# Raw parked operands of x, split on landing, and three more eviction buffers in the last projection phases of a hybrid encoder layer

## The chip, the cores and the metric

The kernel runs on one core of one Trainium2 chip. A core has a matrix engine (PE, with PEld for its weight loads), a vector engine (DVE), a scalar engine (ACT), a general engine (POOL), and a queue processor (SP) that issues the DMA transfers. Each engine works through its own list in order and waits where an instruction's inputs or buffers are not ready. The metric is device time in microseconds, the median of several runs; less is better. Before the change it is 1917.55 us (three runs, 1917.55 to 1919.67).

## What is computed

One layer on 2048 frames of a new stream and on 64 frames that continue another one:

```python
h = rmsnorm(x, norm_g) @ w_in          # x: (T, 1024), w_in: (1024, 6144)
qa, ka, va, za, qb, kb, vb, zb, ga, gb = jnp.split(h, _split_points(), axis=-1)
oa = attention(qa, ka, va)             # two softmaxes, ALiBi, block-causal, a1 - lam * a2
ob = retention(qb, kb, vb)
oa = (rmsnorm(oa, subln_g) * 0.8) * silu(za)
ob = rmsnorm(ob) * silu(zb)
m = ga * (oa @ w_oa) + gb * (ob @ w_ob)
y = x + m @ w_out
```

All data are 32-bit floats. The projection by `w_in` is the largest matrix product. The outputs are `y`, the keys and values, and the retention states.

## The kernel before

**Precision.** PE multiplies operands that are rounded (type fp32r). To keep the precision, an operand is split into a high part (a rounding copy, on ACT) and a low part (operand minus high part, on DVE or POOL), and each product is three matmuls: high by high, high by low, low by high. `xh`, `xl` are the parts of x, `wh`, `wl` those of a weight.

**Stages.** The frames are projected in two halves. The first half runs to some 600 us. In the second half, `w_stream` goes through the weights in order (`natural` for keys, queries and values, then `transposed` for eleven pairs of column blocks), and the last five pairs go through `quad`. Meanwhile `z_stream` runs attention and retention. After quad, the output stage follows (its first matmuls are L2652). In the profile, `transposed` is the matmul of L1131 with 256, 288 or 512 columns, quad is L1547, and attention is L1862 to L1999.

**Quad** multiplies in the manner of Strassen: a 2 x 2 blocked product with seven block products in place of eight. So x's blocks A11, A12, A22 and the sums S1 to S4 of blocks are its operands. `PHASES` (L73) lists the seven in order: t2 with S2, b11 with A11, b21 with A12, t1 with S1, t3 with S3, t4 with A22, b22 with S4. A phase takes one operand of x (high and low part, 1.1 MB each) through the five pairs, for two groups of 256 and 288 columns: ten groups of 12 matmuls, 120 in a phase, 840 in all. Each group ends in one PSUM bank, which ACT (`q_copy`, L1574) or DVE (`q_scaled`, L1567) evicts, either into a sum kept in SBUF (`u`) or into an eviction buffer (`ev`, three of them) that is stored to DRAM (`gaT`, `gbT`). In phase t3 each group has two evictions on DVE.

**Parking.** The operands don't fit beside the rest of the second half. `x_again` writes them to DRAM (`xd`, one tensor of high and one of low parts): first A11, A12, A22, straight from `xh` and `xl`; then, in 20 chunks of 128 or 96 columns, S1 to S4: POOL adds high and low part (L1460) and forms the sums (L1463 to L1469), ACT casts them (L1492, into the one buffer `thi`), DVE subtracts (L1495, in one of the two buffers `tlo`), SP stores both. `x_pass` loads each phase's parts into one of two slots in the room of x's second segment, as soon as a slot is free; the loads stand on L1515, which the trace shows as L279, the helper `ld`. Stores are L284, the helper `st`.

**Weights.** `next_piece` takes a loaded piece of weights (`ws`, three buffers), casts it on ACT (L726), and starts a task `next_low` that subtracts the low part (L741) when the cast is done: on POOL, in quad on the less loaded of DVE and POOL. Then it waits until ACT's planned backlog is at most 0.7 us (`PACE`).

**What sets the order.** A planner runs all these generators as tasks with priorities. It keeps an estimated clock for each engine (`P`, `A`, `V`, `G`, and `ld`, `st` for transfers); a task yields the time at which it wants to go on, and the first ready task of the highest priority goes next. Instructions of PE, ACT and DVE stand in their lists as the tasks emit them; those of POOL and SP are ordered by the framework's scheduler. An estimate that is too short makes an engine wait at that place, with all that is behind it.

## Time and profile before

| | |
|---|---|
| median of three runs | 1917.55 us |
| the profiled execution | 1916.72 us, span 1914.9 us |
| busy: PE, DVE, ACT, POOL | 1879.6, 1327.4, 965.8, 667.3 us |
| PE idle in all | 35.3 us |
| mean granted PE clock | 0.995 |
| DMA | 353.45 MB, mean 185 GB/s |
| quad's matmuls | 1391.3 to 1560.6 us |

The profile is of one execution. A line of waits reads: who waited, for whom, total us, times, longest us. In lists of instructions the brackets at the end give the idle time before one and what ended it. A busy PE can still be slow: the granted clock falls after a pause, and the count of matmuls in a stretch shows that.

### The profile page before, as it was taken

Reading aid. Unit: us, or ns where it says so; the run is one execution under the profiler, and the core shown is the slowest. Engines: PE = TensorE matmul, PEld = TensorE weight load, DVE = VectorE, ACT = ScalarE, POOL = GpSimd, SP = SyncE. Lnnn points to the kernel's source line nnn. Section 1 sums busy time; section 2 is a strip of 40 time slices with the busy share of each in tenths; the row PEclk is TensorE's granted clock in tenths of the full one; section 3 lists DMA queues with packets and bytes.
Section 4 is the critical chain, followed back from the end, with each engine's and each line's share of the span. In section 5 each row is a group of like instructions: output and inputs, shape, how many; then the busy total and the mean of one; then the engine's idle time right before and its main releaser. Section 6 shows DMA issues by size and latency. Waiting matters only on the chain.

```text
span 1914.9 us, 32977 instructions
## 1 busy us (share of the span) xinstructions
PE 1879.6 (98%) x11090; PEld 1652.8 (86%) x11090; DVE 1327.4 (69%) x3089; ACT 965.8 (50%) x2242; POOL 667.3 (35%) x727
## 2 busy tenths in 40 slices
PE   9999999999998999999999999999999999999999
PEld 7788888888888889888888889889999889999887
DVE  6765756656574776876377686668787469987664
ACT  6434544545334666555355554546675246654221
POOL 2420365554651132121402263611022435532442
PEclk9999999999999999999999999999999999999999
DMA  7654456666858886564523764762744989886542
GB/s 252 216 171 135 156 157 192 185 188 198 253 158 245 249 279 186 154 179 124 152 66 105 188 172 130 188 175 73 229 136 123 295 252 288 265 260 199 179 153 78
DMA packets 409755, 353.45 MB, mean 185 GB/s; under 512 B 85617, under 2 KB 355057, under 8 KB 407794
## 3 DMA queue, kind: packets, MB, share of 16 engines
q1 hardware_dynamic: 409586, 351.35, 62.3%
q8 instruction: 88, 1.44, 0.3%
q14 instruction: 81, 0.66, 0.1%
HBM read 224.96 MB, written 125.44 MB: 183 GB/s over the span
## 4 chain that ended last, share of the span: by engine, by line
PE 58%; DMA 5%; DVE 4%; POOL 1%; issue 1%; SPq 1%; ACT 1%; DVEq 0%; POOLq 0%; ACTq 0%
PE mm L1131 19%; PE at L1974 3%; PE s L1863 2%; PE s L1862 2%; PE mm L1547 2%; PE pv L1954 2%; PE pv L1953 2%; PE pv L1952 2%; DMA gbT<-ev 1%; PE s L2776 1%; PE s L2778 1%; PE s L2777 1%; DMA gaT<-ev 1%; DMA xd<-xsl 1%; PE at L2653 1%
## 5 line engine op out<-in xcount | busy, mean ns | idle before, releaser
L741 POOL TENSOR_TENSOR wl<-ws,wh 128x512 fp32r<-128x512 f32 x106 | 140.9, 1340 | 291.6 <-ACT wh L726 204.8
L1131 PE MATMUL mm<-wh,xh 128*128 128x512 f32 x504 | 203.5, 404 | 0.0
L1131 PE MATMUL mm<-wl,xh 128*128 128x512 f32 x504 | 198.0, 393 | 1.1 <-POOL wl L741 1.1
L1131 PE MATMUL mm<-wh,xl 128*128 128x512 f32 x504 | 198.2, 393 | 0.0
L1131 PE MATMUL mm<-xh,wh 128*128 128x288 f32 (+2 forms) x544 | 180.3, 332 | 5.8 <-ACT ev L1574 5.8
L1131 PE MATMUL mm<-xh,wl 128*128 128x288 f32 (+2 forms) x544 | 176.4, 324 | 0.0
L1131 PE MATMUL mm<-xl,wh 128*128 128x288 f32 (+2 forms) x544 | 176.3, 324 | 0.0
L1902 ACT ACTIVATE row<-row,a_mx 128x1024 f32<-128x1024 f32 (+7 forms) x144 | 149.9, 1043 | 12.6 <-DVE a_mx L1881 12.6
L1990 DVE TENSOR_TENSOR atl<-at,ath 128x512 fp32r<-128x512 f32 (+1 forms) x144 | 92.6, 658 | 82.6 <-ACT ath L1988 82.2
L1988 ACT CAST ath<-at 128x512 fp32r<-128x512 f32 (+1 forms) x144 | 79.2, 564 | 116.0 <-PE at L1974 108.7
L850 POOL TENSOR_TENSOR wl<-ws,wh 128x256 fp32r<-128x256 f32 x64 | 54.2, 846 | 195.9 <-ACT wh L841 195.8
L1871 DVE CUSTOM_DVE_ANT_0 row<-s,dfar 128x512 f32<-128x512 f32 (+2 forms) x150 | 92.7, 632 | 42.2 <-PE s L1863 41.7
L1728 POOL TENSOR_TENSOR r_y<-r_y,r_sq 128x256 f32<-128x256 f32 x32 | 27.2, 849 | 264.6 <-DVE r_sq L1725 191.4
L1131 PEld LDWEIGHTS mm<-xh,wh 128*128 128x128 f32 x544 | 103.0, 189 | 12.8 <-ACT ev L1574 6.0
L1131 PEld LDWEIGHTS mm<-wh,xl 128*128 128x128 f32 x504 | 94.6, 188 | 21.6
L1131 PEld LDWEIGHTS mm<-wl,xh 128*128 128x128 f32 x504 | 95.0, 189 | 19.2 <-POOL wl L741 1.9
L1131 PEld LDWEIGHTS mm<-wh,xh 128*128 128x128 f32 x504 | 94.8, 188 | 17.6 <-DVE raw L1302 0.2
L1131 PEld LDWEIGHTS mm<-xh,wl 128*128 128x128 f32 x544 | 103.0, 189 | 7.0 <-POOL wl L741 0.3
L1131 PEld LDWEIGHTS mm<-xl,wh 128*128 128x128 f32 x544 | 103.2, 190 | 6.5
L1924 DVE SCALAR_TENSOR_TENSOR row<-row,a_w 128x1024 f32<-128x1024 f32 (+5 forms) x88 | 99.5, 1137 | 0.0
L1862 PE MATMUL s<-K,q 128*128 128x512 f32 (+3 forms) x246 | 93.1, 380 | 0.3 <-DVE a_acc L1871 0.2
L1863 PE MATMUL s<-K,q 128*128 128x512 f32 (+3 forms) x246 | 89.7, 365 | 0.0
(541 smaller groups left out, 6044.4 us busy)
## 6 DMA issues: line engine op xcount, KB each, us to landing
ws<-in_w_in_dram SPq DMA_DIRECT2D x155, 256.0 KB, 3.6
q<-qT SPq DMA_DIRECT2D x128, 128.0 KB, 3.1
K<-kT SPq DMA_DIRECT2D x48, 256.0 KB, 4.7
V<-vN SPq DMA_DIRECT2D x24, 512.0 KB, 5.2
row<-in_x_prompt_dram SPq DMA_DIRECT2D x16, 512.0 KB, 4.7
wz<-in_w_in_dram SPq DMA_DIRECT2D x32, 256.0 KB, 4.3
row<-in_cache_k_T_dram SPq DMA_DIRECT2D x32, 256.0 KB, 3.0
row<-in_cache_v_diff_dram SPq DMA_DIRECT2D x32, 256.0 KB, 3.6
```

What stands on the lines that cost most here:

```text
L741: eng.tensor_sub(l, st, h.bitcast(F32))
L850: nc.gpsimd.tensor_sub(l[:, cs], src, h[:, cs].bitcast(F32))
L1131: nc.tensor.matmul(ps, p, q, start=c == 0 and i == 0, stop=c == KC - 1 and i == 2)
L1547: nc.tensor.matmul(ps, w[:, c], x, start=c == 0 and k == 0, stop=c == 3 and k == 2)
L1862: nc.tensor.matmul(ps, q1s, kk, start=True, stop=False)
L1863: nc.tensor.matmul(ps, q2s, kk, start=False, stop=True)
L1871: nc.vector.tensor_tensor_reduce(out=row[:, k0:k0 + n], in0=ps, in1=tab, scale=-SLOPES[h], scalar=3.0e38, op0=ALU.add, op1=ALU.min, accum_ ...
L1902: nc.scalar.activation(u, u, AF.Exp, bias=mx, scale=-1.0, accum_out=lp[:, k:k + 1])
L1924: nc.vector.scalar_tensor_tensor(out=u0, in0=u1, scalar=w[:, 0:1], in1=u0, op0=ALU.mult, op1=ALU.add)
L1974: nc.tensor.transpose(at[:, w:w + 128], src, self.ident)
L1988: nc.scalar.copy(ah[:, :w], at[:, :w])
L1990: nc.vector.tensor_sub(al[:, :w], at[:, :w], ah[:, :w].bitcast(F32))
```

## The change

It edits four things.

- **Parking.** Only S2 is still split before it is stored (`xd2`). S1, S3, S4, A22, A11 and A12 are stored unsplit (`xd`, six parcels in place of twice seven). A chunk now takes one `tlo` buffer for the blocks and the `thi` buffer for the sums, both filled by POOL; ACT and DVE split S2 alone, a quarter of the elements, into an eviction buffer. A chunk's task rests 4000 ns of the planner's time (`SPREAD`) before the next.
- **Landing.** S2 is loaded in two parts into slot 0 before quad. Every other operand is loaded unsplit into `xraw`, a new buffer in the room where the sums `u` are (11 blocks of each width remain in place of 13 and 12), and then split into a slot: four casts on ACT and four subtractions on DVE, 544 columns each. The next raw load waits until this is done.
- **Eviction buffers.** Once parking is over, `q_ev` takes from `ev`, `thi` or `tlo`, whichever is free first: six buffers.
- **Weights.** Outside quad the low part is emitted on POOL right behind the cast, and the next piece is not paced.

```diff
 
 PLAIN = 11
+SPREAD = 4000.0
...
-NAMES = ("S1", "S3", "S2", "S4", "A11", "A12", "A22")
+NAMES = ("S1", "S3", "S4", "A22", "A11", "A12")
...
-        self.xd = [tc.dram_tile([128, 7, 4, 544], F32, name=f"xd{j}") for j in range(2)]
+        self.xd = tc.dram_tile([128, 6, 4, 544], F32, name="xd")
+        self.xd2 = tc.dram_tile([128, 2, 4, 544], F32, name="xd2")
...
         self.wq += new
-        self.spawn(self.next_low(st, h, l, t, new, kind), 0, "w")
-        yield self.act - PACE
-
-    def next_low(self, st, h, l, t, new, kind):
+        if kind == "quad":
+            self.spawn(self.next_low(st, h, l, t, new), 0, "w")
+            yield self.act - PACE
+        else:
+            self.next_sub(self.nc.gpsimd, self.G, st, h, l, t, new)
+            yield self.pe
+
+    def next_low(self, st, h, l, t, new):
         yield t - LAT
-        eng, cost = self.lighter() if kind == "quad" else (self.nc.gpsimd, self.G)
+        self.next_sub(*self.lighter(), st, h, l, t, new)
+
+    def next_sub(self, eng, cost, st, h, l, t, new):
         eng.tensor_sub(l, st, h.bitcast(F32))
         t = cost(512, t)
         self.give("ws", t)
         for u in new:
             u[2] = t
-        yield self.pe
...
+    def x_chunk(self, g, c, raw, sums, a, n):
         xh, xl = self.xnext[g]
-        for k, (b, j) in enumerate(((1, 1), (1, 0), (0, 0), (0, 1))):
+        for k, (b, j) in enumerate(((1, 0), (1, 1), (0, 0), (0, 1))):
             h, l = (x[:, b, 4 * j + c, a:a + n].bitcast(F32) for x in (xh, xl))
             nc.gpsimd.tensor_add(raw[:, k], h, l)
             t = self.G(n, self.pe)
-        s1, s3, s2, s4 = (raw[:, k] for k in range(4))
-        nc.gpsimd.tensor_add(s1, s1, s3)
+        a21, a22, a11, a12 = (raw[:, k] for k in range(4))
+        s1, s3, s4, s2 = (sums[:, k] for k in range(4))
+        nc.gpsimd.tensor_add(s1, a22, a21)
         self.G(n)
-        nc.gpsimd.tensor_sub(s3, s2, s3)
+        nc.gpsimd.tensor_sub(s3, a11, a21)
         self.G(n)
-        nc.gpsimd.tensor_sub(s2, s1, s2)
+        nc.gpsimd.tensor_sub(s2, s1, a11)
         self.G(n)
-        nc.gpsimd.tensor_sub(s4, s4, s2)
-        return self.G(n)
+        nc.gpsimd.tensor_sub(s4, a12, s2)
+        return t, self.G(n)
 
     def x_again(self):
...
         yield lambda: "nat1" in self.done
-        self.kept = 0
         for g, w in enumerate(WIDTH):
-            gsl = slice(256 * g, 256 * g + w)
-            for k, (b, j) in (("A11", (0, 0)), ("A12", (0, 1)), ("A22", (1, 1))):
-                for x, d in zip(self.xnext[g], self.xd):
-                    self.kept = self.st(d[:, NAMES.index(k), :, gsl], x[:, b, 4 * j:4 * j + 4, :].bitcast(F32), 600000)
-                    yield self.pe + 4000
             n = (128, 96)[g]
             for c, a in [(c, a) for c in range(4) for a in range(0, w, n)]:
                 yield from self.take("tlo")
-                l = self.sb(self.ep, [128, 512], "tlo", "xsl", F32R)[:, 0:4 * n]
-                raw = l.bitcast(F32)
-                t = self.x_chunk(g, c, raw.rearrange("p (k t) -> p k t", k=4), a, n)
+                yield from self.take("thi")
+                raw, sums = (self.sb(self.ep, [128, 512], tag, name)[:, 0:4 * n].rearrange("p (k t) -> p k t", k=4)
+                             for tag, name in (("tlo", "xa"), ("thi", "xs")))
+                t, t2 = self.x_chunk(g, c, raw, sums, a, n)
+                usl = slice(256 * g + a, 256 * g + a + n)
                 yield t
-                yield from self.take("thi")
-                h = self.sb(self.ep, [128, 512], "thi", "xsh", F32R)[:, 0:4 * n]
-                nc.scalar.copy(h, raw)
-                t = self.A(4 * n, self.pe)
+                t = self.st(self.xd[:, 3:6, c, usl], raw[:, 1:4], n << 11)
+                yield t2
+                ev, tag = yield from self.q_ev(2 * n)
+                e = ev.bitcast(F32R).rearrange("p (k t) -> p k t", k=2)
+                nc.scalar.copy(e[:, 0], sums[:, 3])
+                t3 = self.A(n, self.pe)
+                self.give("tlo", max(t, t2))
+                t4 = self.st(self.xd[:, 0:3, c, usl], sums[:, 0:3], n << 11)
+                yield t3
+                nc.vector.tensor_sub(e[:, 1], sums[:, 3], e[:, 0].bitcast(F32))
+                t = self.V(n + 100, t3)
+                self.give("thi", max(t, t4))
                 yield t
-                nc.vector.tensor_sub(l, raw, h.bitcast(F32))
-                t2 = self.V(4 * n + 100, t)
-                for d, x, tag, t in zip(self.xd, (h, l), ("thi", "tlo"), (t, t2)):
-                    if t > self.pe:
-                        yield t
-                    self.kept = self.st(d[:, 0:4, c, 256 * g + a:256 * g + a + n],
-                                        x.bitcast(F32).rearrange("p (k t) -> p k t", k=4), n << 11)
-                    self.give(tag, self.kept)
+                self.kept = self.st(self.xd2[:, :, c, usl], e.bitcast(F32), n << 10)
+                self.give(tag, self.kept)
+                yield self.pe + SPREAD
         self.parked = 1
 
     def x_pass(self):
-        self.xslots, self.xfree, self.parked = [], [(0, 0.0), (1, 0.0)], -1
+        self.xslots, self.xfree, self.parked, self.xraw = [], [(1, 0.0)], -1, None
         yield lambda: self.parked == 1 and self.seg1_done is not None
         yield max(self.seg1_done, self.kept)
-        for _, name, _ in PHASES:
+        for k, (_, name, _) in enumerate(PHASES):
+            if k == 0:
+                for j, x in enumerate(self.x_slot(0)):
+                    t = self.ld(x.bitcast(F32), self.xd2[:, j].rearrange("p c t -> p (c t)"), 1114112)
+                self.xslots.append((0, t))
+                yield lambda: self.xraw is not None
+                continue
+            t = self.ld(self.xraw, self.xd[:, NAMES.index(name)].rearrange("p c t -> p (c t)"), 1114112)
             s = yield from self.ring(self.xfree)
-            for x, d in zip(self.x_slot(s), self.xd):
-                t = self.ld(x.bitcast(F32), d[:, NAMES.index(name)].rearrange("p c t -> p (c t)"), 1114112)
-                yield self.pe
+            yield t
+            h, l = self.x_slot(s)
+            for c in range(0, 2176, 544):
+                self.nc.scalar.copy(h[:, c:c + 544], self.xraw[:, c:c + 544])
+                t = self.A(544, self.pe)
+                yield t
+                self.nc.vector.tensor_sub(l[:, c:c + 544], self.xraw[:, c:c + 544], h[:, c:c + 544].bitcast(F32))
+                t = self.V(644, t)
             self.xslots.append((s, t))
+            yield t
 
     def u_room(self):
...
         pool = self.z2.enter_context(self.tc.tile_pool(name="sums", bufs=1))
-        room = [pool.tile([128, 2304], F32, tag=f"u{k}", name=f"u{k}") for k in range(3)]
-        self.ufree = [[(x[:, n * k:n * k + n], 0.0) for x in rooms for k in range(x.shape[1] // n)]
-                      for n, rooms in ((256, (room[0], room[2][:, 0:1152])), (288, (room[1], room[2][:, 1152:2304])))]
+        self.xraw = pool.tile([128, 2176], F32, tag="xraw", name="xraw")
+        self.ufree = []
+        for n in WIDTH:
+            u = pool.tile([128, 11 * n], F32, tag=f"u{n}", name=f"u{n}")
+            self.ufree.append([(u[:, n * k:n * k + n], 0.0) for k in range(11)])
...
     def q_ev(self, n):
-        yield from self.take("ev")
-        return self.sb(self.ep, [128, 512], "ev")[:, :n]
+        tag = yield from self.either(1, "ev", *(("thi", "tlo") if self.parked == 1 else ()))
+        return self.sb(self.ep, [128, 512], tag, "ev")[:, :n], tag
...
     def q_end(self, q, ps, bank, k, t, dst, b, scale, grouped):
-        ev = yield from self.q_ev(q["n"])
+        ev, tag = yield from self.q_ev(q["n"])
...
-        self.q_put(q, dst, ev, b, grouped)
+        self.q_put(q, dst, ev, tag, b, grouped)
...
-        self.give("ev", self.st(out, ev[:, 0:256], 1 << 17))
+        self.give(tag, self.st(out, ev[:, 0:256], 1 << 17))
```

The lists are the same up to about 600 us, and hold the same matmuls behind. Three places show what moves.

*DVE, the end of attention in quad.* `atl` is the low part of attention's weights, `u` and `ev` are quad's evictions (into a sum, into a buffer). Before:

```order
L1990 TENSOR_TENSOR atl_17201<-at_17195,ath_17200 128x512
L1731 SCALAR_TENSOR_TENSOR r_o_17001<-r_o_17001,gsub_754,r_y_17003 128x256
L1990 TENSOR_TENSOR atl_17227<-at_17221,ath_17226 128x512
L1567 TENSOR_TENSOR ev_17238<-tp_17205,u2_16006 128x256
L1990 TENSOR_TENSOR atl_17253<-at_17247,ath_17252 128x512
L1990 TENSOR_TENSOR atl_17275<-at_17270,ath_17274 128x384
L1567 TENSOR_TENSOR ev_17284<-mm_17256,u2_16006 128x288
L1567 TENSOR_TENSOR u2_16006<-mm_17297,u0_16004 128x256
L1692 TENSOR_TENSOR r_sq_17316<-r_sq_17316,pv_17087 1x256
```

After:

```order
L1534 TENSOR_TENSOR xl1_124<-xraw_16428,xh1_123 128x544
L2012 TENSOR_TENSOR atl_16936<-at_16930,ath_16935 128x512
L1534 TENSOR_TENSOR xl1_124<-xraw_16428,xh1_123 128x544
L1589 TENSOR_TENSOR u256_16429<-tp_16916,u256_16429 128x256
L2012 TENSOR_TENSOR atl_16970<-at_16964,ath_16969 128x512
L2012 TENSOR_TENSOR atl_16986<-at_16980,ath_16985 128x512
L1589 TENSOR_TENSOR u288_16430<-mm_16949,u288_16430 128x288
L2012 TENSOR_TENSOR atl_17020<-at_17014,ath_17019 128x512
L2012 TENSOR_TENSOR atl_17034<-at_17029,ath_17033 128x384
L1589 TENSOR_TENSOR u256_16429<-mm_16995,u256_16429 128x256
```

The last `atl` (128x384) stood among the evictions into `ev` of phase b21; it stands now among those into `u` of phase b11, beside the split of an operand (L1534). In PE's list the last transposition of attention (L1974, now L1996) stands after 174 of quad's 840 matmuls, before after 354; 486 of its 544 stand ahead of quad, before 444.

*ACT, the last chunks of parking* (`ath` is attention's high part). Before:

```order
L1574 COPY ev_14208<-mm_14169 128x288
L1492 CAST xsh_14217<-xsl_14174 128x384
L1574 COPY ev_14251<-mm_14213 128x288
L1988 CAST ath_14292<-at_14287 128x512
L1492 CAST xsh_14296<-xsl_14264 128x384
L1988 CAST ath_14303<-at_14298 128x512
L1988 CAST ath_14339<-at_14334 128x512
L1988 CAST ath_14354<-at_14349 128x512
```

After:

```order
L1596 COPY ev_14776<-mm_14664 128x288
L1924 ACTIVATE row_6182,a_lp_14795<-row_6182,a_mx_14712 128x1024
L1924 ACTIVATE row_6182,a_lp_14795<-row_6182,a_mx_14712 128x640
L1498 CAST ev_14808<-xs_14763 128x96
L1706 COPY r_o_14813<-pv_14605 128x256
L1708 ACTIVATE r_sq_14814<-r_o_14813 128x256
L1710 ACTIVATE r_hi_14816<-r_o_14813 128x256
L1924 ACTIVATE row_6182,a_lp_14822<-row_6182,a_mx_14792 128x1024
```

The casts of four sums at once (`xsh`), which need the one buffer `thi`, are gone from between attention's casts; one cast of 96 columns into an eviction buffer is left of a chunk.

*DVE and SP in phase t3 of quad.* Before, DVE, then SP:

```order
L1567 TENSOR_TENSOR u0_16004<-s_17616,u0_16004 128x256
L1567 TENSOR_TENSOR ev_17669<-s_17616,u2_16006 128x256
L1567 TENSOR_TENSOR u1_16005<-s_17637,u1_16005 128x288
L2598 TENSOR_TENSOR on_17478<-on_17478,z_17479 128x528
L1567 TENSOR_TENSOR ev_17689<-s_17637,u1_16005 128x288
L1567 TENSOR_TENSOR u0_16004<-at_17660,u0_16004 128x256
L1567 TENSOR_TENSOR ev_17708<-at_17660,u0_16004 128x256
L1567 TENSOR_TENSOR u1_16005<-at_17682,u1_16005 128x288
L2609 TENSOR_TENSOR ogl_17681<-on_17478,ogh_17680 128x528
L1567 TENSOR_TENSOR ev_17733<-at_17682,u1_16005 128x288
```

```order
L279 DMA z_17569<-zaT_67 128x2x264
L279 DMA xh1_123<-xd0_76 128x2176
L279 DMA xl1_124<-xd1_77 128x2176
L279 DMA ws_17565<-wsum_75 128x4x128
L279 DMA on_17568<-oaT_71 128x2x264
L284 DMA gaT_69<-ev_17557 128x256
L279 DMA z_17592<-zbT_68 128x2x264
L279 DMA on_17591<-obT_72 128x2x264
L284 DMA gaT_69<-ev_17583 128x4x8
L284 DMA gaT_69<-ev_17583 128x256
```

After, DVE, then SP:

```order
L1589 TENSOR_TENSOR u256_16429<-mm_17623,u256_16429 128x256
L1534 TENSOR_TENSOR xl1_124<-xraw_16428,xh1_123 128x544
L1589 TENSOR_TENSOR ev_17655<-mm_17623,u256_16429 128x256
L1589 TENSOR_TENSOR u288_16430<-s_17646,u288_16430 128x288
L2620 TENSOR_TENSOR on_17507<-on_17507,z_17508 128x528
L1534 TENSOR_TENSOR xl1_124<-xraw_16428,xh1_123 128x544
L1589 TENSOR_TENSOR ev_17680<-s_17646,u288_16430 128x288
L1589 TENSOR_TENSOR u256_16429<-s_17669,u256_16429 128x256
L2482 TENSOR_TENSOR w_o_diffl0_17240<-wst_17580,w_o_diffh0_17239 128x2x256
L1534 TENSOR_TENSOR xl1_124<-xraw_16428,xh1_123 128x544
L1589 TENSOR_TENSOR u288_16430<-at_17697,u288_16430 128x288
L2631 TENSOR_TENSOR ogl_17685<-on_17507,ogh_17684 128x528
```

```order
L280 DMA ws_17630<-wsum_75 128x4x128
L280 DMA wst_17643<-in_w_o_ret_dram 128x2x256
L280 DMA wst_17656<-in_w_o_ret_dram 128x2x256
L280 DMA wst_17681<-in_w_o_diff_dram 128x2x256
L285 DMA gaT_69<-ev_17655 128x256
L280 DMA ws_17704<-wsum_75 128x4x128
L280 DMA ws_17725<-wsum_75 128x4x128
L285 DMA gaT_69<-ev_17680 128x4x8
L285 DMA gaT_69<-ev_17680 128x256
```

Between t3's evictions there are now the splits of the operand for t4 (L1534), and more low parts of the output weights (L2482, before L2460, behind t3): to its last eviction the list of t3 holds 20 evictions, four splits, six low parts of the output weights and two operations of the gates. On SP the pair of loads `xh`, `xl` between the stores of evictions is gone. The store of `ev_17655` stands behind the load of `wst_17681`, whose buffer is freed by the low part of `wst_17580`, six operations behind that eviction on DVE.

9 lines of the change are left out of this document (4 added, 5 removed).

## The prediction

> **What bounds the kernel now.** The page's first part comes first.
>
> ```profile
> PE 1879.6 (98%) x11090; PEld 1652.8 (86%) x11090; DVE 1327.4 (69%) x3089; ACT 965.8 (50%) x2242; POOL 667.3 (35%) x727
> ```
>
> The matrix engine (PE) is busy for 1879.6 of 1914.9 us and the change takes no product away. So only PE's 35.3 us of idle time can be won, and the slow clock that follows a long pause. I therefore asked for busy time by stage. The columns are length, then busy time of PE, PEld, DVE, ACT and POOL (instructions in brackets), PE's granted clock, DMA share and GB/s.
>
> ```profile
> 1100.00:1265.00 165.00, 158.00 (x1078) 146.00 (x1077) 109.52 (x270) 83.40 (x194) 86.69 (x154) 0.99 0.64 167
> 1265.00:1391.00 126.00, 125.94 (x842) 116.42 (x842) 100.81 (x290) 77.23 (x159) 17.76 (x15) 0.99 0.56 156
> 1391.00:1495.00 104.00, 102.45 (x786) 99.30 (x785) 82.21 (x207) 64.44 (x137) 29.01 (x24) 1.00 0.45 141
> 1495.00:1515.00 20.00, 20.00 (x162) 20.00 (x161) 9.97 (x19) 6.96 (x11) 10.14 (x7) 1.00 1.00 328
> 1515.00:1562.00 47.00, 37.75 (x258) 36.17 (x258) 27.70 (x49) 14.95 (x26) 13.05 (x11) 0.89 0.88 248
> 1562.00:1915.00 353.00, 349.10 (x2231) 316.63 (x2230) 259.28 (x408) 152.40 (x353) 144.52 (x108) 1.00 0.67 206
> ```
>
> Operands are parked in the first row, quad runs from 1391 to 1561. Its tail, after attention, loses most: 258 matmuls in 47 us, where the row above does 162 in 20 us (8.1 per us). At that rate 258 take 31.9 us, so the tail loses **15.1 us**: 9.25 us idle (47 - 37.75), 5.9 us slow clock. The parking stage is idle for 7.0 us. The chain of waits names the cause in the tail (start, length, what; the second row is SP's own, from the timeline):
>
> ```profile
> by line: DMA gbT<-ev 70.8%; PE s L1547 12.5%; SPq L279 7.1%; DVE ev L1567 7.0%; DVE u L1567 4.3%; DVE ogl L2609 3.8%; issue 3.1%; SPq L284 2.8%; DVEq L1567 0.6%
> ...
> 1521.49 1.85 SPq L279 DMA_DIRECT2D xl<-xd  x1
> ...
> 1523.43 8.51 DMA gbT<-ev
> 1532.07 0.47 DVE ev L1567
> ```
>
> From 1514 to 1540, 71% of the chain is a store of an eviction. The worst took 8.51 us from its issue, straight behind a load that SP issued at 1521.49, the second half of an operand of x. The next rows are DMA issues of 1490 to 1562 (count, KB, median us to landing), then waits of 1520 to 1562 (total, times, longest):
>
> ```profile
> gbT<-ev SPq DMA_DIRECT2D x23, 128.0 KB, 3.3
> xh<-xd SPq DMA_DIRECT2D x2, 1088.0 KB, 7.8
> xl<-xd SPq DMA_DIRECT2D x2, 1088.0 KB, 9.4
> ...
> DVE ev L1567 <- DMA gbT<-ev: 15.9, 9, 5.7
> ...
> PE s L1547 <- DVE ev L1567: 4.9, 2, 3.2
> ...
> PE s L1547 <- DVE wl L741: 2.5, 1, 2.5
> ```
>
> DVE waits nine times for one of three buffers to be stored, PE for DVE. The weight's low part on DVE is late for the same reason: it stands in DVE's list behind those evictions.
>
> **Parking.** PE's waits from 1100 to 1265, and the ACT instructions at the longest of them:
>
> ```profile
> PE pv L1952 <- ACT ath L1988: 3.4, 1, 3.4
> PE pv L1954 <- DVE atl L1990: 2.0, 2, 1.7
> PE s L2319 <- DMA row<-kbT: 1.0, 1, 1.0
> ...
> 1260.44 0.51 ACT L1492 CAST xsh<-xsl 128x384 fp32r<-128x384 f32 x1 [5.20 <-DMA xd<-xsh]
> 1260.86 1.06 ACT L1988 CAST ath<-at 128x512 fp32r<-128x512 f32 x2
> ...
> 1134.95 1.70 DVE L1495 TENSOR_TENSOR xsl<-xsl,xsh 128x512 fp32r<-128x512 f32 x1
> ...
> 1260.00:1270.00 10.00, 8.29 (x48) 7.60 (x49) 6.54 (x18) 4.07 (x9) 0.00 (x0) 0.83 0.23 61
> ```
>
> ACT stood 5.20 us before a parking cast whose one buffer was still being stored, with attention's cast behind it: 3.4 us of PE. The 1.7 us wait is the 1.70 us subtraction of a parked sum on DVE. After the pause the clock is 0.83 for 10 us, about 1.7 us more. I put parking at 3.4 + 1.7 + 1.7 = 6.8 us, and the stage with its small waits at 8.7.
>
> **The change, part by part.** *Stores of A11, A12, A22 leave* and come back as raw sums with the chunks. The traffic halves: 14 parcels of 1.1 MB were stored and loaded, now 8. The removed early stores surround this stall, which I leave in place:
>
> ```profile
> 606.56 0.61 PE L1131 MATMUL mm<-xh,wh 128*128 128x288 f32 x1 [5.78 <-ACT ev L1574]
> ...
> 598.82 3.12 SPq L279 DMA_DIRECT2D q<-qT  x4
> 602.04 0.54 SPq L284 DMA_DIRECT2D qbT<-ev  x1
> ```
>
> Its eviction's store is issued only at 602.04, behind loads of q that still stand in front of it. I take 0; the bounds are 0 and -5.8.
>
> *Splits while parking.* These are 20 casts on ACT and 20 subtractions on DVE, on a quarter of the elements now:
>
> ```profile
> L1492 ACT CAST xsh<-xsl x20: 495/516/635, 1073.6 to 1260.4; 128x384 fp32r<-128x384 f32 x12, 128x512 fp32r<-128x512 f32 x8
> L1495 DVE TENSOR_TENSOR xsl<-xsl,xsh x20: 546/622/1700, 1074.6 to 1263.5; 128x384 fp32r<-128x384 f32 x12, 128x512 fp32r<-128x512 f32 x8
> ```
>
> That is 10.3 us of ACT and 12.4 us of DVE by medians. With a quarter of the elements and some fixed part I estimate half, so 5 and 6 us go. ACT no longer waits there for a 4-operand store: the wait for the buffer moves to POOL's sums, behind which weights' low parts are queued. And each chunk holds one of the three eviction buffers for its split sum. Each chunk also rests 4 us of the planner's time. I take half of the 8.7 us as saved: **-4.3** (bounds 0 and -8.7).
>
> *Splits on landing.* Six operands, each four ACT casts and four DVE subtractions of 544 columns, 24 each. By the rows above (512 columns: ACT 0.62, DVE 0.62 to 1.70) that is 24 x 0.65 = 15.6 us of ACT and 16 to 41 us of DVE. DVE is 79% busy from 1391 to 1495 (82.21 of 104); four operands there would add at least 10 us. But attention's last transposition now stands after 174 of quad's 840 matmuls in PE's list, where it stood after 354, so less of it overlaps. In the tail, the crowded phase is t3. Its list on DVE has 20 evictions, four splits, six low parts of the output weights and two gate operations:
>
> ```profile
> L2460 DVE TENSOR_TENSOR w_o_diffl<-wst,w_o_diffh 128x512 fp32r<-128x512 f32 x5 | 6.5, 1295 | 0.0
> ...
> L2460 DVE TENSOR_TENSOR w_o_retl<-wst,w_o_reth 128x512 fp32r<-128x512 f32 x5 | 4.8, 982 | 0.0
> ...
> L1567 DVE TENSOR_TENSOR ev<-at,u 128x256 f32<-128x256 f32 (+1 forms) x10 | 4.3, 434 | 2.8 <-DMA gbT<-ev 2.8
> ...
> L2598 DVE TENSOR_TENSOR on<-on,z 128x528 f32<-128x528 f32 x4 | 2.8, 698 | 0.0
> ```
>
> The last numbers before the second bar are the mean ns of one. Evictions 20 x 0.434 = 8.7, splits 2.6 to 6.8, low parts 6 x 1.14 (mean of the two rows) = 6.8, gates 1.4: 19 to 24 us against 120 matmuls at 8.1 per us, 14.8 us. DVE falls 5 to 9 us behind. Six PSUM banks at 1.48 us each give 8.9 us of cover, and t4 has half the evictions, so DVE catches up. With the cover gone, PE waits for the rest. I take **+2** for both places (bounds 0 and +9).
>
> The longest DVE splits above, 1.70 against 0.69 us, run while POOL works. [...]
>
> *Operand loads and eviction buffers in quad.* Each load of a raw operand is half of what the phase had, 1.1 MB, and evictions may use the three parking buffers too. A group ends each 1.48 us, so a buffer returns after six groups, 8.9 us, where it had 4.4. Even the 8.51 us store fits, and its load in front is half as long. I take 12 of the 15.1 us as saved, **-12** (bounds -15.1 and -6); the other 3 us are for weights: SP is held up there too.
>
> ```profile
> SPq L279 <- POOL wl L741: 55.7, 19, 7.0
> ```
>
> *Low parts of W at once, no pacing.* Same instructions on the same POOL: 0 of themselves. They reshuffle PE's list from about 600 us on. Of the 35.3 us of idle time, 7.0, 0.1, 1.6, 9.3 and 3.9 lie in the six stages above and 5.8 in the stall at 606; the 7.6 left are drawn anew: 0, within 4 us either way.
>
> **Sum.** -4.3 + 2 - 12 = -14.3 us. The profiled run took 1916.72 us (span 1914.9), so 1902.4; the median of the runs is 0.8 us higher, and the forecast is **1903.5 us**.
>
> **Rivals.** *SP, not the buffers, holds the tail.* Stores queue in SP's one list behind loads of weights that wait for their buffers (55.7 us above). For it: in the new order a t3 store stands behind a load whose buffer only DVE frees six operations later. Against: the wait counted is DVE for the store's landing. Half the tail is saved: 1917.55 - 7.5 - 4.3 + 2 = 1908.
>
> *The buffers do nothing*, because DVE is the next bound in the tail: +9 eats most of the 12. 1917.55 - 12 - 4.3 + 9 = 1910 at best; with the parking gain gone too, 1915: no change to speak of.
>
> *Slower: attention is packed too tightly.* The planner, freed of the splits, sets attention earlier in PE's list, by 354 - 174 = 180 matmuls or 22 us at 8.1 per us; 486 of its 544 transpositions now precede quad, not 444. From 1100 to 1391 DVE works 210 of 291 us; in 22 us less that is 78%, and its waits are in order. For it: single late ACT or DVE results cost 3.4 and 1.7 us here, and each pause over 3 us costs clock. Against: from 1265 to 1391, at 80% DVE, PE idles 0.06 us. At three times today's 8.7 us it costs 17.4 more instead of saving 4.3, and with +9 for the splits 1917.55 - 12 + 17.4 + 9 gives 1932. It decides once that stage loses over 19 us (8.7 + 12 - 2).
>
> [...]
>
> **How the numbers follow.** The forecast has 0.5 (own range 1894 to 1907), SP 0.2 (1907 to 1912), the buffers for nothing 0.1 (1910 to 1919), slower 0.2 (from 1920 to 1935). The low end is all of 15.1 + 8.7 saved, 1894. The upper end reaches into the slower case, to 1924, leaving under 0.2 out. No change is within 0.2% (3.8 us), about what a measurement can tell. Faster: 0.5 + 0.2 + 0.03; same 0.07; slower 0.2.
>
> **What would show it.** Right: from the end of attention to the end of quad PE holds 8 matmuls per us at clock 1.00, DVE's waits for stores of ga and gb fall below 3 us, DMA moves some 13 MB less, and no ACT cast of parking precedes a wait of attention. Wrong: PE waits for ev or weights remain in the tail, splits on DVE of 1.7 us stand before PE waits, or PE idles over 10 us between 1100 and 1391.

## The result and the profile after

The changed kernel takes 1904.54 us (median of six runs, 1899.9 to 1906.59). The kernel before took 1918.95 us beside it (1917.55 to 1921.13). The ratio is **0.9922**, with a 95% interval of 0.9908 to 0.9935: 14.4 us less. The profiled execution took 1899.9 us (span 1897.5), which is the fastest of the six. It lies 4.6 us under its median, and the profiled execution of the kernel before 2.2 us under the median above. So 2.4 us of the difference between the two traces is only which executions were traced.

From the page after, the engines' line and the DMA total:

```profile
PE 1871.9 (99%) x11090; PEld 1649.4 (87%) x11090; DVE 1336.5 (70%) x3112; ACT 973.7 (51%) x2266; POOL 670.7 (35%) x728
...
DMA packets 402876, 340.09 MB, mean 179 GB/s; under 512 B 85649, under 2 KB 348945, under 8 KB 401682
```

PE is idle for 25.6 us (1897.5 - 1871.9) in place of 35.3, and its busy time is 7.7 us shorter for the same 11090 matmuls. Those 7.7 us aren't work saved. In the stretches where the granted clock is 0.50, PE was busy for 16.6 us before and is for 9.2 us after. Behind the stall at 606 us, matmuls of 128x288 start 0.24 us apart at 0.50, and 0.13 us apart from 613 on, at 1.00. From this ratio, or from the 0.50 itself, I estimate that the clock makes 3.3 to 3.7 of the 7.7 us; the rest stays open. 13.4 MB less are moved.

Busy time by stage, with the columns of the table in the prediction. Attention's last transposition now starts at 1454.0 (before, 1482.9), and quad runs from 1410.2 to 1544.2:

```profile
1100.00:1265.00 165.00, 159.35 (x1106) 148.73 (x1105) 111.72 (x320) 90.57 (x215) 74.46 (x131) 0.99 0.62 167
1265.00:1410.00 145.00, 145.00 (x965) 133.98 (x964) 120.83 (x337) 88.27 (x184) 20.56 (x22) 1.00 0.41 113
...
1454.00:1500.00 46.00, 46.00 (x368) 45.83 (x367) 36.55 (x58) 26.22 (x50) 26.19 (x17) 1.00 0.84 246
1500.00:1515.00 15.00, 12.01 (x92) 11.39 (x91) 15.00 (x23) 8.48 (x16) 9.06 (x8) 1.00 0.91 270
1515.00:1544.20 29.20, 29.20 (x229) 28.71 (x228) 19.66 (x36) 8.68 (x15) 14.70 (x11) 1.00 1.02 268
```

The tail of quad (the last three rows) has no idle time but 3.0 us from 1500 to 1515, where DVE is busy for all 15.00 us. Before, 9.25 us were idle there, at clock 0.89. The parking stage (first row) still loses 5.65 us, where it lost 7.0.

What PE waits for in the tail, from 1454 to 1545 (total, times, longest):

```profile
PE at L1569 <- DVE ev L1589: 2.4, 2, 1.4
PE s L1569 <- DVE ev L1589: 0.6, 1, 0.6
```

The same for the parking stage, 1100 to 1265:

```profile
PE s L2341 <- DMA row<-kbT: 2.9, 1, 2.9
PE pv L1974 <- ACT ath L2010: 1.9, 1, 1.9
...
```

And DVE's waits from 1400 to 1600 for eviction buffers:

```profile
DVE ev L1589 <- DMA gbT<-ev: 2.1, 3, 1.1
...
DVE ev L1589 <- DMA gaT<-ev: 1.5, 1, 1.5
```

Over the same stretch before:

```profile
DVE ev L1567 <- DMA gbT<-ev: 18.8, 11, 5.7
...
DVE ev L1567 <- DMA gaT<-ev: 6.7, 2, 5.3
```

So DVE waits 3.6 us (2.1 + 1.5) for eviction buffers to be stored, and waited 25.5 us before (18.8 and 6.7). PE's 3.0 us of waits in the tail are for DVE, which has its own work to do. The chain of waits of 1496 to 1520 shows that work:

```profile
1499.53 1.10 DVE on L2620
1500.63 0.74 DVE xl L1534
...
1503.08 0.90 DVE w_o_diffl L2482
...
1505.33 1.72 DVE ogl L2631
...
1508.24 1.48 DVE xl L1534
...
1510.45 1.56 DVE w_o_retl L2482 x2
```

These are a gate (`on`, `ogl`), splits on landing (`xl`) and low parts of the output weights, between the evictions of phase t3: the list that the prediction added up.

The stall at 606 us stayed at 6.1 us (5.78 before):

```profile
606.58 0.61 PE L1138 MATMUL mm<-xh,wh 128*128 128x288 f32 x1 [6.11 <-ACT ev L1596]
```

The two traces part by 17.4 us of span. From attention's end to the program's end the span is 443.52 us, and 432.05 before. Behind that point the kernel now has 180 more of quad's matmuls. At 3.01 us for 24, as blocks of 24 follow one another in the chain of waits, these are 22.6 us. So the stretch is 11.1 us shorter for the same work, and 6.3 us were won earlier.

### The profile page after: what moved, and what is told of

It is laid out like the page before. It is cut to its first block, busy times and chain, and to the rows that moved or that the text cites. A ratio compares the mean times of both kernels' runs of the same rounds, so it can differ in the third digit from the quotient of the medians.

```text
span 1897.5 us, 33103 instructions
## 1 busy us (share of the span) xinstructions
PE 1871.9 (99%) x11090; PEld 1649.4 (87%) x11090; DVE 1336.5 (70%) x3112; ACT 973.7 (51%) x2266; POOL 670.7 (35%) x728
## 4 chain that ended last, share of the span: by engine, by line
PE 88%; DVE 5%; DMA 4%; issue 1%; ACT 1%; SPq 1%; POOL 1%; DVEq 0%; ACTq 0%
PE mm L1138 29%; PE mm L990 8%; PE tp L990 4%; PE at L1996 3%; PE s L1884 2%; PE s L1885 2%; PE s L990 2%; PE mm L1569 2%; PE pv L1976 2%; PE pv L1975 2%; PE pv L1974 2%; PE s L2800 1%; PE s L2799 1%; PE s L2798 1%; SPq L280 1%
## 5 line engine op out<-in xcount | busy, mean ns | idle before, releaser
L749 POOL TENSOR_TENSOR wl<-ws,wh 128x512 fp32r<-128x512 f32 x107 | 149.6, 1409 | 251.8 <-ACT wh L728 243.9
L1893 DVE CUSTOM_DVE_ANT_0 row<-s,dfar 128x512 f32<-128x512 f32 (+2 forms) x149 | 91.3, 629 | 35.5 <-PE s L1885 35.3
L1138 PEld LDWEIGHTS mm<-wh,xh 128*128 128x128 f32 x504 | 94.8, 188 | 17.4 <-DVE raw L1309 0.2
L1884 PE MATMUL s<-K,q 128*128 128x512 f32 (+3 forms) x243 | 91.6, 379 | 0.4 <-DVE a_acc L1893 0.4
L728 ACT CAST wh<-ws 128x512 fp32r<-128x512 f32 x111 | 67.0, 619 | 41.6 <-PE mm L1569 8.4
```

Of the source, the lines that this page charges most:

```text
L728: self.nc.scalar.copy(h, st)
L749: eng.tensor_sub(l, st, h.bitcast(F32))
L1138: nc.tensor.matmul(ps, p, q, start=c == 0 and i == 0, stop=c == KC - 1 and i == 2)
L1884: nc.tensor.matmul(ps, q1s, kk, start=True, stop=False)
L1893: nc.vector.tensor_tensor_reduce(out=row[:, k0:k0 + n], in0=ps, in1=tab, scale=-SLOPES[h], scalar=3.0e38, op0=ALU.add, op1=ALU.min, accum_ ...
```

## The experiments

Every kernel is compared with the kernel before on the same chip. The chips differ by a microsecond or two (on three of them the kernel before has medians of 1916.53, 1916.56 and 1918.14), so I compare ratios. The changed kernel's own is 0.9922. The last three columns are PE's idle time in the profiled execution, in us (length less busy time of three stretches): the stall at 606 is in the first, parking and most of attention in the second, quad in the third.

| kernel | what differs | median us (range) | ratio [95%] | 550-1000 | 1000-1400 | 1400-1560 |
|---|---|---|---|---|---|---|
| before | | 1918.95 (1917.55-1921.13) | 1 | 10.5 | 7.4 | 10.8 |
| after | | 1904.54 (1899.9-1906.59) | 0.9922 [0.9908, 0.9935] | 9.8 | 5.7 | 3.2 |
| b_6buf | before, six buffers | 1911.51 (1910.34-1914.01) | 0.9973 [0.9963, 0.9984] | 10.9 | 7.3 | 6.0 |
| a_3buf | after, three buffers | 1913.36 (1908.81-1917.71) | 0.9982 [0.9971, 0.9994] | 10.2 | 6.0 | 13.1 |
| a_2loads | after, a second load before each split | 1924.15 (1923.43-1928.24) | 1.0040 [1.0028, 1.0052] | 8.5 | 8.4 | 16.7 |
| a_3buf_2loads | both of these | 1927.08 (1922.02-1935.24) | 1.0053 [1.0035, 1.0071] | 10.8 | 9.9 | 19.1 |
| a_dump | after, copies of 1.1 MB, not tied to quad | 1906.83 (1905.16-1907.98) | 0.9948 [0.9936, 0.9960] | 9.8 | 7.2 | 6.1 |
| a_3buf_dump | the same, three buffers | 1912.50 (1908.65-1918.68) | 0.9980 [0.9971, 0.9989] | 8.9 | 6.4 | 11.6 |
| a_dump2 | after, the second halves' bytes in quad | 1907.34 (1906.20-1910.43) | 0.9947 [0.9935, 0.9960] | 10.8 | 5.7 | 5.6 |
| a_early6 | after, six buffers at 606 us too | 1905.59 (1902.34-1909.97) | 0.9945 [0.9933, 0.9957] | 9.2 | 6.2 | 5.6 |
| a_nospread | after, parking steps close together | 1899.10 (1898.32-1903.64) | 0.9915 [0.9903, 0.9927] | 9.9 | 3.3 | 5.1 |
| a_paced | after, weights spawned and paced as before | 1903.78 (1903.19-1905.60) | 0.9926 [0.9914, 0.9939] | 11.3 | 2.8 | 7.7 |
| a_splitpool | after, low halves on POOL | 1907.58 (1904.94-1912.78) | 0.9943 [0.9930, 0.9957] | 10.5 | 9.0 | 7.8 |
| a_nospread_etlo | after, close steps, S2's split in its own tile | 1898.41 (1896.19-1902.40) | 0.9900 [0.9886, 0.9914] | 9.3 | 1.8 | 4.4 |

One row measures the comparison itself. In a_early6 a few evictions near 606 us may use other buffers. Its lists of PE and DVE are those of the changed kernel, instruction for instruction, and ACT's differ by the place of one eviction. Yet it gave 0.9945, against runs of the kernel before beside it, 0.0023 (4.4 us) above the changed kernel's 0.9922, and its trace loses 5.6 us in quad in place of 3.2:

```profile
PE at L1569 <- DVE ev L1589: 5.4, 2, 3.6
```

So a difference of 0.0025 between two rows, or of 2 to 3 us in a column, can come without any edit in that place. It also matters which execution was traced: the changed kernel's lies 4.6 us under its median, that of a_splitpool 5.2 over it, that of a_3buf_2loads 8.2 over it.

PE's list is the same in five of the kernels, so their traces can be compared from one instruction on. From attention's last transposition to the program's end they take 443.5 us (after), 446.7 (a_early6), 447.8 (a_dump2), 449.8 (a_splitpool) and 454.6 (a_3buf).

### The buffers, alone and taken away

The theory was that the six buffers make the tail's gain (B); the rival, that the halved loads do (L). One kernel gives the kernel before six buffers and nothing else, one takes the three extra buffers from the changed kernel:

```diff
 # b_6buf, from the kernel before
-        yield from self.take("ev")
-        return self.sb(self.ep, [128, 512], "ev")[:, :n]
+        tag = yield from self.either(1, "ev", *(("thi", "tlo") if self.parked == 1 else ()))
+        return self.sb(self.ep, [128, 512], tag, "ev")[:, :n], tag
...
 # a_3buf, from the changed kernel
-        tag = yield from self.either(1, "ev", *(("thi", "tlo") if self.parked == 1 else ()))
+        tag = yield from self.either(1, "ev")
```

> The kernel before with one part of the change alone: evictions may take the parking buffers too once parking is over, six in all. Theory B: the waits for stores in quad's tail vanish, 9 to 12 us less, 1907 to 1910 us. Theory L: stores stay long behind 2.2 MB loads, part of the waits remains, 1912 to 1916 us.

> The changed kernel, but evictions take only the three buffers ev, as before; loads stay halved. If the buffers bring the gain (theory B), DVE waits for stores of ga and gb again in quad's tail, 8 us or more in total, and the time is about 1913 us, 9 above the changed kernel. If the halved operand loads bring it (theory L), a store now lands in some 3 us behind a short load, three buffers (4.4 us for three groups) are nearly enough, and the time stays within 4 us of the changed kernel, 1902 to 1908.

Alone the buffers bring 0.0027 x 1917 = 5.2 us (3 to 7 by the interval). Taken from the changed kernel they cost 0.9982 - 0.9922 = 0.0060, 11.5 us; against a_early6 it is 0.0037, 7.1 us. The traces say the same from attention's last transposition on: 11.1 and 7.8 us. Without the buffers, only 3.5 us of the change are left. PE's waits in quad with the buffers taken away (1400 to 1570), where PE's list is the same as in the changed kernel and those of DVE and ACT differ in part:

```profile
PE s L1569 <- DVE ev L1589: 6.4, 3, 3.1
PE at L1569 <- DVE ev L1589: 5.2, 3, 2.5
PE mm L1569 <- DVE ev L1589: 1.3, 2, 0.8
```

PE waits 12.9 us for evictions, which the changed kernel does for 3.0 and a_early6 for 5.4. That confirms B for the mechanism. But the buffers alone bring less, 5.2 us. The chain of waits in the kernel before with six buffers says what is late next:

```profile
1522.35 8.40 DMA gbT<-ev
1531.95 0.63 DVE on L2598
1532.83 4.04 DMA wst<-in_w_o_diff_dram
1537.18 4.33 DMA wst<-in_w_o_diff_dram
1541.57 4.79 DMA ws<-in_w_in_dram
...
```

The 8.40 us store is still there, and behind it three loads of weights follow one another almost to the end of quad. PE's waits for evictions fell from 4.9 to none in quad's own products, and its waits for high parts of weights rose from 0.8 to 3.2 us. The measured 1911.51 lies between what the two theories expected.

### The bytes of the operands

To put the second 1.1 MB of each operand back, I first loaded it into the room of the low part, ahead of the split:

```diff
 # a_2loads, from the changed kernel; a_3buf_2loads has the edit of a_3buf too
             s = yield from self.ring(self.xfree)
-            yield t
             h, l = self.x_slot(s)
+            t = self.ld(l.bitcast(F32), self.xd[:, NAMES.index(name)].rearrange("p c t -> p (c t)"), 1114112)
+            yield t
```

> The changed kernel with six eviction buffers, but ahead of each of the six raw loads a second parcel of 1.1 MB is loaded into the low part's room (the split overwrites it), so that a phase's load is 2.2 MB again; the result stays the same. Theory B: six buffers cover the longer stores, the time stays within 4 us of the changed kernel, and only the split is later. Theory L: stores take up to 8 us behind the loads, DVE waits for them, about 1912 us.

> The changed kernel with three eviction buffers and 2.2 MB of loads in each phase, so both gains are taken back at once while parking and weights stay changed. Both theories: the tail of quad loses as much as before the change, 12 to 15 us, and the time is 1914 to 1918 us. If it stays under 1910, neither is the cause, and the gain comes from the order of attention and quad.

Both are slower than the kernel before, and for another reason than either theory. In a_2loads PE waits in quad for this:

```profile
PE s L1570 <- DVE xl L1535: 7.7, 5, 4.0
PE at L1570 <- DVE xl L1535: 5.0, 2, 3.0
```

The extra load may only start when a slot is free, and the split waits for it. So the low part is late by a whole transfer (its median from issue to landing is 7.7 us). It is a miss as a test of the bytes. It shows what the landing's cover is worth instead: a late split costs 22.6 us against the changed kernel (1.0040 - 0.9922 = 0.0118) and 18.2 against a_early6, with an order of PE that is in part another one.

The second try was a copy from DRAM to DRAM that nothing waits for:

```diff
 # a_dump, from the changed kernel; a_3buf_dump has the edit of a_3buf too
             t = self.ld(self.xraw, self.xd[:, NAMES.index(name)].rearrange("p c t -> p (c t)"), 1114112)
+            self.ld(self.xdump[:, k].rearrange("p c t -> p (c t)"), self.xd[:, NAMES.index(name)].rearrange("p c t -> p (c t)"), 1114112)
```

> The changed kernel, with the bytes of the parked operands' second halves put back on the queues: beside each load of an unsplit operand a copy of the same 1.1 MB from DRAM to DRAM, which nothing waits for, so that the split isn't later by it. Theory L (the halved loads carry what the buffers alone don't): with six buffers the stores' delay is partly covered, so 2 to 5 us over the changed kernel's 1904.5: 1906 to 1910. Theory B (only the buffers count, the rest of the gain lies before the attention's end): 1904 to 1905.

> The same extra copies with three eviction buffers in place of six. Theory L: the loads and the buffers relieve the same store, so with neither the tail is as it was before the change, 8 us or more over the 1913.4 that three buffers alone gave, about 1918 to 1922. Theory B: no more than three buffers alone, 1912 to 1915.

1906.83 looks like theory L and 1912.50 like theory B, but neither says anything of the bytes. Since nothing held the copies, all six were issued before quad began:

```profile
L280 SPq DMA_DIRECT2D xdump<-xd x6: 476/530/617, 1269.5 to 1291.5; - x6
```

They did shift the planner's clock, and with it PE's list. So a_dump is 0.0026 above the changed kernel with a new order and no byte more in quad. As a_early6 lies 0.0023 above it with the old order, that difference isn't shown to be the order's either.

The third try holds the bytes in place: the landed raw operand is stored to DRAM after its first piece is split. The lists of PE, DVE and ACT are those of the changed kernel.

```diff
 # a_dump2, from the changed kernel
                 t = self.V(644, t)
+                if c == 0:
+                    self.st(self.xdump[:, k].rearrange("p c t -> p (c t)"), self.xraw)
```

> The changed kernel with the bytes of the second halves put back at the time at which the kernel before moved them: once the first piece of a landed raw operand is split, the raw operand is also stored to DRAM (1.1 MB), which nothing but the next raw load waits for. The order of the work on TensorE, VectorE and ScalarE stays as it is. Theory L (in the tail the queues are full, and half of the operands' bytes less lets weights and stores through earlier): the gain of the tail falls back to about what six buffers alone gave in the kernel before (0.9973), so a ratio of 0.995 to 0.9975, 1909 to 1912 where the kernel before takes 1916.5, with TensorE waiting for weights (L728, L749) or for evictions again between 1470 and 1560 us. Theory B (the buffers cover late stores, and the bytes don't matter): 0.992 to 0.9935, 1901 to 1904.

0.9947 lies between the theories' ranges, at the edge of L's. It is 0.0025 (4.8 us, 1 to 8 by the intervals) above the changed kernel, but only 0.0002 above a_early6, which has the same lists and none of these bytes. From attention's last transposition on it takes 4.3 us more than the changed kernel, and 1.0 more than a_early6. So the runs don't show that the bytes cost anything; they leave room for nothing and for some 8 us. PE's waits in quad:

```profile
PE s L1572 <- DVE ev L1592: 2.7, 2, 1.8
PE at L1572 <- ACT wh L729: 2.5, 1, 2.5
```

The window of 1500 to 1550, which had 47.01 us of busy PE and clock 1.00 in the changed kernel, and 44.57 us and 0.97 in a_early6:

```profile
1500.00:1550.00 50.00, 44.57 (x333) 43.36 (x332) 38.45 (x64) 21.95 (x40) 26.80 (x19) 0.97 1.02 303
```

The waits for evictions are 2.9 us in all (3.0 in the changed kernel, 5.4 in a_early6, which loses as much here). The new one is 2.5 us for the high part of a weight; in the chain of waits its cast stands behind a load of output weights that takes 4.64 us to land. So with six buffers the bytes may reach PE by the weights, as in b_6buf. That is one wait of one profile: a_dump, without the bytes in quad, has a wait of 2.5 us for `wh` too. Neither the cost of the bytes nor its path is shown.

### The stall at 606 us

```diff
 # a_early6, from the changed kernel
-        tag = yield from self.either(1, "ev", *(("thi", "tlo") if self.parked == 1 else ()))
+        tag = yield from self.either(1, "ev", *(("thi", "tlo") if self.parked == 1 or self.nplain == 1 else ()))
```

> The changed kernel, with the six eviction buffers allowed also in the stretch around 606 us, where six A-blocks are stored and the evictions of the plain stage wait. Theory: the 6.1 us that TensorE waits there for the eviction at L1596 is a wait for one of three buffers, and the clock's dip behind it (0.93 in 600 to 650 us) follows from it; then the wait falls under 1 us and the time is 6 to 8 us under the changed kernel's 1904.5, about 1897. Rival: the stores themselves are what is late (the transfers of the A-blocks hold every queue), so that three more buffers only put the wait off; then TensorE still waits 4 us or more between 590 and 640 us and the time is within 2 us of 1904.5.

The rival holds: no gain (0.9945, and nothing in its lists accounts for the 0.0023 above the changed kernel). The wait for the eviction is gone, and this stands in its place between 590 and 650:

```profile
PE tp L1884 <- DMA q<-qT: 4.2, 1, 4.2
```

PE gets past the eviction and then waits for a load of attention's queries. From 590 to 640 it is busy for 43.20 us, and 42.69 in the changed kernel; the DMA queues are 95% busy there. In that place the transfers are what is late, and buffers only choose who waits.

### Parking and the order before attention's end

```diff
 # a_nospread, from the changed kernel
-SPREAD = 4000.0
+SPREAD = 0.0
 # a_nospread_etlo has this too
-                ev, tag = yield from self.q_ev(2 * n)
+                tag = "tlo"
+                yield from self.take(tag)
+                ev = self.sb(self.ep, [128, 512], tag, "xe")[:, :2 * n]
```

> The changed kernel with its parking steps one right behind the other (SPREAD 0 in place of 4000), so that the parking lies as close together as in the kernel before. Theory: the spreading carries what is left of the parking's gain, so that close steps bring back 3 to 5 us of waits before the attention: 1907 to 1910. Rival: what holds the attention's start is that the split of S2 and the evictions ask for the same three buffers, however far apart the steps are; then the time stays within 2 us of 1904.5, and the waits for ath (L2010) at 1200 to 1250 us stay at 2 to 3 us.

> The changed kernel with parking steps close together and S2's two halves in a tile of their own, so that parking and evictions don't ask for the same buffers. If that competition is what is left of the parking's cost (2.8 to 2.9 us in each of 1100 to 1150 and 1200 to 1250 us in the changed kernel), both go and the time is 3 to 6 us under the changed kernel's: a ratio of 0.9885 to 0.9905. If an edit like this only deals the order of the work anew, it falls anywhere within 4 us of it: 0.990 to 0.9945.

The spreading brings nothing: without it the ratio is 0.9915. My theory expected 1907 to 1910 and got 1899. The rival's time, within 2 us of 1904.5, holds by the ratio (1902.6), but not its waits for `ath`. In a_nospread PE's only listed wait from 1100 to 1265 is this one, and the 1.9 us for `ath` are gone:

```profile
PE s L2341 <- DMA row<-qbT: 2.3, 1, 2.3
```

With S2's split in a tile of its own as well, the stretch of 1000 to 1400 loses 1.8 us (before 7.4, after 5.7), and the median is the lowest of all kernels, 1898.41. Its interval (0.9886 to 0.9914) overlaps that of the changed kernel. It lies in both expected ranges, so I can't say that it is faster than the changed kernel. And since a_nospread had lost the wait without the separate tile, it doesn't show that the competition for buffers was the cause either.

```diff
 # a_paced, from the changed kernel
-        if kind == "quad":
-            self.spawn(self.next_low(st, h, l, t, new), 0, "w")
-            yield self.act - PACE
-        else:
-            self.next_sub(self.nc.gpsimd, self.G, st, h, l, t, new)
-            yield self.pe
+        self.spawn(self.next_low(st, h, l, t, new, kind), 0, "w")
+        yield self.act - PACE
```

> The changed kernel with the low parts of the weights ahead of the last product spawned and paced as before the change. Expected by the term of nought, plus or minus 4: a ratio of 0.990 to 0.9945, 1897 to 1906 where the kernel before takes 1916.5. Rival (weights at once carry a part of the gain): over 0.9945, with waits of TensorE for wl before 1400 us that the changed kernel doesn't have.

0.9926: the weights at once are worth nothing that can be measured, as the term of nought said. But where the time lies has changed. The two windows in which the changed kernel loses 2.87 and 2.78 us are full, and quad loses 4.5 us more (2.0 more than in a_early6):

```profile
1100.00:1150.00 50.00, 50.00 (x368) 47.48 (x368) 40.54 (x109) 28.47 (x70) 22.98 (x39) 1.00 0.47 131
1200.00:1250.00 50.00, 50.00 (x351) 46.75 (x350) 28.23 (x79) 23.61 (x57) 27.56 (x44) 1.00 0.88 225
```

### The splits on landing

```diff
 # a_splitpool, from the changed kernel
-                self.nc.vector.tensor_sub(l[:, c:c + 544], self.xraw[:, c:c + 544], h[:, c:c + 544].bitcast(F32))
+                self.nc.gpsimd.tensor_sub(l[:, c:c + 544], self.xraw[:, c:c + 544], h[:, c:c + 544].bitcast(F32))
```

> The changed kernel with the low halves of the split on landing subtracted by GpSimd in place of VectorE, all else in the same order. A piece of 128x544 takes VectorE 0.71 to 1.87 us; GpSimd takes some 1.5 us by its 128x512 pieces. If the split's cost is VectorE's time in the stretch where it is the bound (1499 to 1513 us), 2 to 4 us are gained: 1900 or a ratio of 0.990. If the cost is how late the split ends (4 pieces, each 0.8 us later), TensorE waits for the low parts instead and the time rises by 3 to 15 us, a ratio of 0.9935 to 1.0.

On PE, DVE and ACT the rest of the list stands as it was. The ratio is 0.9943, 4 us above the changed kernel's and the same as a_early6's 0.9945. So there is no gain, though 24 instructions have left the engine that is the bound in t3; that the edit costs time isn't shown by the ratio. From attention's last transposition on it takes 6.3 us more than the changed kernel and 3.0 more than a_early6. The groups of DVE from 1410 to 1560 (busy, mean ns of one), first of the changed kernel, then with the splits on POOL:

```profile
L2620 DVE TENSOR_TENSOR on<-on,z 128x528 f32<-128x528 f32 x9 | 8.1, 901 | 1.7 <-DMA gbT<-ev 1.7
...
L2482 DVE TENSOR_TENSOR w_o_diffl<-wst,w_o_diffh 128x512 fp32r<-128x512 f32 x5 | 5.9, 1186 | 0.0
L2631 DVE TENSOR_TENSOR ogl<-on,ogh 128x528 fp32r<-128x528 f32 x4 | 4.7, 1171 | 0.0
L2482 DVE TENSOR_TENSOR w_o_retl<-wst,w_o_reth 128x512 fp32r<-128x512 f32 x5 | 4.5, 905 | 0.0
```

```profile
L2620 DVE TENSOR_TENSOR on<-on,z 128x528 f32<-128x528 f32 x9 | 9.4, 1043 | 4.5 <-ACT z L2617 2.8 <-DMA gbT<-ev 1.8
...
L2482 DVE TENSOR_TENSOR w_o_diffl<-wst,w_o_diffh 128x512 fp32r<-128x512 f32 x5 | 6.9, 1377 | 0.0
L2482 DVE TENSOR_TENSOR w_o_retl<-wst,w_o_reth 128x512 fp32r<-128x512 f32 x5 | 6.8, 1376 | 0.0
L2631 DVE TENSOR_TENSOR ogl<-on,ogh 128x528 fp32r<-128x528 f32 x4 | 6.5, 1618 | 0.0
```

The same 23 instructions take 29.6 us in place of 23.2. With the splits on DVE they take 26.9 in a_early6 and 22.3 in a_dump2, so 3 to 7 us more are the edit's. The 24 splits took DVE 27.1 us and take POOL 35.1. So a tenth to a quarter of the 27.1 us that left DVE came back: these instructions were slower with POOL busy for 100.22 us of 1400 to 1560 in place of 70.39, as the splits themselves were beside POOL's work (below). PE also waits 1.7 us for a split's high part in this profile, which it doesn't in the changed kernel. What each is worth in time isn't settled. The 9.0 us in the column of 1000 to 1400 are no part of it: no split on landing runs there, and the lists are those of the changed kernel (5.7). So that column differs by some 3 us between executions of one order.

## Why the prediction was right, and where its steps were off

1903.5 us was forecast (its own sum is nearer 1903.2) and 1904.5 came. The sign holds, and of the largest term the part of the buffers is shown; that of the halved loads is not. Not every term had its size.

- **Operand loads and eviction buffers, -12.** Together with the +2 of the splits this made -10. The tail is 11.1 us shorter between the traces, and 7.9 us by that of a_early6. Taking the buffers away gives back 7 to 11.5 us. The store's wait was read rightly, and its price within these bounds. What the step didn't tell is that buffers alone bring 5.2 us: the weights behind the same stores come next. The step had kept 3 us back for weights; with the buffers alone the weights hold more than that, and in the traces of the changed kernel and a_early6 none keeps PE waiting in the tail. Whether that is for the halved loads or for the rest of the change stays open.
- **Splits on landing, +2.** The list of t3 was forecast to take DVE 19 to 24 us against 14.8 of matmuls, with most of it covered. DVE is busy for all of 1500 to 1515 and PE loses 3.0 us (5.4 in a_early6). The 24 subtractions take 27.1 us, between the 16 and 41 that were the bounds. Their group (busy us, mean ns of one):

```profile
L1534 DVE TENSOR_TENSOR xl<-xraw,xh 128x544 fp32r<-128x544 f32 x24 | 27.1, 1128 | 0.0
```

  And their shortest, median and longest duration in ns:

```profile
L1534 DVE TENSOR_TENSOR xl<-xraw,xh x24: 707/720/1872, 1420.1 to 1529.4; 128x544 fp32r<-128x544 f32 x24
```

  Some take 0.71 and some 1.87 us. The prediction's 41 us are 24 times the 1.70 us of the longest split while parking; the trace has 27.1. In it the 11 splits of 1.42 us and more all began while an instruction of POOL was running, which went on for 0.84 us or more; of the 13 of 0.71 to 0.72 us nine met none, and four began 0.03 us before one of POOL ended, within 0.02 us of its start (two), or 0.39 us ahead of it. The run with the splits on POOL agrees: the 23 instructions of DVE above took 29.6 us there, and 22.3 to 26.9 with the splits on DVE.
- **Parking, -4.3.** This step was mis-sized in the changed kernel: the stage's idle time went from 7.0 to 5.65 us, so 1.35 in place of about 4. In a_early6 and a_dump2, with the same lists, the stage is idle for 6.2 and 5.7 us at a mean clock of 0.98 (0.99 before), so the gain is not clear of nothing. The step had said that each chunk holds one of the three eviction buffers, and had taken the half for want of a row. The row is there now: ACT stands 8.72 us before an eviction and 3.07 before the split of S2, both for a buffer to be stored, with the casts of attention behind them.

```profile
1221.03 0.40 ACT L1596 COPY ev<-mm 128x288 f32<-128x288 f32 x1 [8.72 <-DMA zbT<-ev]
1221.32 1.08 ACT L2010 CAST ath<-at 128x512 fp32r<-128x512 f32 x2
1225.47 0.27 ACT L1498 CAST ev<-xs 128x96 fp32r<-128x96 f32 x1 [3.07 <-DMA xd<-ev]
```

  What was meant to go (a cast of parking before a wait of attention) is gone in that form, and an eviction stands in its place. In three other orders of the same parking (a_nospread, a_paced, a_nospread_etlo) the stretch of 1000 to 1400 loses only 1.8 to 3.3 us, so the halved parking may allow more than the changed kernel's order gets. How much of the measured 14.4 us is parking stays open. Ahead of attention's end 6.3 us were won between the traces (some 3 by that of a_early6), and 2.4 us of the 17.4 is the choice of executions.
- **Early stores leave, 0.** The stall at 606 stayed, as said, and a_early6 shows why more than a buffer is late there.
- **Weights at once, 0 within 4.** a_paced differs from the changed kernel by 0.0004.
- **The rivals.** SP holding the tail is what b_6buf looks like, with weights late in the queue. In the changed kernel it doesn't come to that; that the halved bytes are the reason isn't shown. DVE as next bound is what happened in t3, at 3.0 us (5.4 in a_early6) and not at 9. The attention packed too tightly did not turn: PE idles 0 us from 1265 to 1410, at 83% of DVE (120.83 of 145).
- **What would show it.** From 1454 to 1500 there are 368 matmuls in 46 us, 8.0 per us, at clock 1.00, but from 1500 to 1515 only 92 in 15 us. The DMA total fell by 13.4 MB. DVE's waits for eviction buffers were to fall below 3 us and fell to 3.6 (6.5 in a_early6). Of the signs against, waits of PE for `ev` remain, at 3.0 us, and splits of 1.48 us and more stand ahead of them.

That the sum came out within 1 us is partly luck: the parking term missed by some 3 us in its stage, the tail by about one the other way, and practically the same lists gave a ratio 4.4 us higher in a_early6.

## What to carry to other kernels

Where buffers wait for stores, count the groups that a buffer may be away against the longest store, and look at what stands behind the same queue: buffers alone gave 5.2 us here, and taking them from the changed kernel cost 7 to 11.5. A larger operand may be split on landing if its load can start a phase ahead: late by one transfer it cost 18 to 23 us here. When edits are worth a few microseconds, run a kernel with the same lists a second time before a difference is put down to an edit: a_early6 lies 4.4 us above the changed kernel, and the 4 to 5 us of a_dump2 and a_splitpool are hardly more than that. Compare traces from one instruction on where the lists are the same.
